# Other SBUF addresses for the split weights, and one queue for the first load and the last store

## The chip, the cores and the metric

The kernel runs on one core of one Trainium2 chip. The metric is the device time of one execution in microseconds; the time before is the median of 3 runs. One core has five engines that run side by side: TensorE (PE in the profile, with its weight loads as PEld), VectorE (DVE), ScalarE (ACT), GpSimd (POOL) and SyncE (SP). Transfers between HBM and SBUF are issued from SP and from ACT and run on 16 DMA engines. SBUF has 128 partitions; an address here is a byte offset within a partition.

## The reference, cut to what matters

```
h = rmsnorm(x) ; proj = h @ w_in                     # 1024 -> q,k,v (512 each), pool (512), gates (2048)
attn   = block attention over q, k, v                # 8 heads of 64; at 256 tokens it is causal attention
pooled = causal means over 2, 4, 8, 16 tokens, one 128x128 map for each of 4 groups, a scale
mixed  = gate0 * (attn @ w_branch_attn) + gate1 * (pooled @ w_branch_pool)
x = x + mixed @ w_out
up = causal_conv3(rmsnorm(x) @ w_up) ; gate, val = split(up)     # 1024 -> 2 x 2816
out = x + (silu(gate) * val) @ w_down                # 2816 -> 1024
```

There are 256 tokens, all in float32.

## The kernel before

**Products.** Each large matrix product is made of three matmuls of type float32r: an operand is split into a high part (`high`, a copy on ACT) and a low part (`low`, the difference, on DVE), and `mm3` adds high x high, high x low and low x high. The weights come in 58 chunks of up to 128 x 2048 numbers (1 MB), in the order that the list `order` writes down: q, k, v, the pool's and the gates' parts, the two branch products, `w_out`, and then `w_up` and `w_down` in turns. `load` fetches a chunk into one of four `raw` buffers from SP's queue; the two q chunks come with x in the tile `xq`. ACT writes the high part into a tile of the pool `whi` and DVE the low part into a tile of `wlo` (four tiles each, taken round by chunk number).

**Matmuls.** In `project` (q, k, v) the activations are the stationary operand, which is loaded into TensorE, and 512 columns of weights stream through as the moving operand: 144 matmuls. In all other float32r products (`feature_tile`, `branch`, `tile_part`, `down`) the weights are stationary and 256 columns of activations (one per token) stream: 2,460 matmuls, of which 1,056 are `w_up`'s (tiles `ps_up`) and 528 are `w_down`'s (tiles `ps_d`). Every matmul has its own weight load, of 128 columns. The remaining 86 matmuls are plain float32 (warm-up, transposes, scores, values, sums).

**Order.** The program order of each engine is fixed by the code; there is no scheduler. All loads stand on SP's queue in one row. The first load is `xq`, in pieces that end after 1, 2, 4, 6 and 8 of the 8 row blocks (`XCUTS`). At the end the eight output blocks of `out_T` are written one after the other, each when DVE has added the residual.

**Addresses.** A tile's address follows from the sizes of what was allocated ahead of it. In the built program all `raw`, `whi` and `wlo` tiles begin at 448 modulo 512, and all activations that a float32r matmul reads (`xhi`, `xlo`, `poolh`, `ath`, `mh`, `hhi`, `ah` and their low parts) at 480. A column slice of either always begins at a multiple of 512 bytes from its tile's start. So the activations stand 32 bytes past the weights, modulo 512, in all 2,604 float32r matmuls.

Of the kernel before, what the change touches and what calls it, by code (L numbers as in the profile page):

```python
# [8 lines left out]
F32 = mybir.dt.float32  # L9
F32R = mybir.dt.float32r  # L10
# [4 lines left out]
P = 128  # L15
S = 256
NT = S // P
D = 1024
KD = D // P
H = 8  # L20
DH = 64
AW = H * DH
# [10 lines left out]
CH = 2048  # L33
# [19 lines left out]
FFN_AHEAD = 6  # L53
KREADY = 0
FIRST = 2
XCUTS = (1, 2, 4, 6, 8)


@with_exitstack
def hybrid_layer_kernel(ctx: ExitStack, tc: tile.TileContext, xq_d, par_d, wkv_d, wpg_d,  # L60
                        wpool_d, wba_d, wbp_d, wout_d, wup_d, wdn_d, out_d):
    nc = tc.nc

    const = ctx.enter_context(tc.tile_pool(name="const", bufs=1))
    raw_p = ctx.enter_context(tc.tile_pool(name="raw", bufs=RAWBUFS))
    whi_p = ctx.enter_context(tc.tile_pool(name="whi", bufs=WBUFS))
    wlo_p = ctx.enter_context(tc.tile_pool(name="wlo", bufs=WBUFS))
    act = ctx.enter_context(tc.tile_pool(name="act", bufs=1))
# [10 lines left out]
    def high(hi, src, scale=1.0):  # L79
        nc.scalar.activation(hi, src, AF.Copy, scale=scale)  # L80
# [16 lines left out]
    order = [("q", None)] * 2 + [("k", wkv_d[c]) for c in range(2)]  # L97
# [10 lines left out]
    raws, his, los = {}, {}, {}  # L108
# [14 lines left out]
    def raw(c, sl):  # L123

        return xq[:, 4 * c + sl.start // 512, S:] if order[c][0] == "q" else raws[c][:, sl]
# [10 lines left out]
    def oldest():  # L136

        return next((c for c in range(len(order)) if c not in spent), len(order))

    def next_high():  # L140
        if at[0] < len(pieces):
            c, sl, first, _ = pieces[at[0]]
            if c - oldest() >= WBUFS:
                return
            at[0] += 1
            if first:
                his[c] = whi_p.tile([P, CH], F32R, tag="whi", name=f"hi_{order[c][0]}{c}")
                los[c] = wlo_p.tile([P, CH], F32R, tag="wlo", name=f"lo_{order[c][0]}{c}")
            high(his[c][:, sl], raw(c, sl))

    def next_low(eager=False):
# [9 lines left out]
    def ahead(upto=0):  # L161

        next_high()
        next_low()
        if at[1] - sum(p[0] < used[0] for p in pieces) < upto:
            next_high()
            next_low()
# [10 lines left out]
    nc.vector.memset(ones, 1.0)  # L178


    xq_all = act.tile([P, KD + KD * (S + AW)], F32, name="xq")
    gmix = xq_all[:, 0:KD]
    xq = xq_all[:, KD:].rearrange("p (k c) -> p k c", c=S + AW)
    xT = xq[:, :, 0:S]
# [5 lines left out]
    cut = 0  # L190
    for k in XCUTS:
        end = KD + k * (S + AW)
        if k == 1:

            nc.scalar.dma_start(out=xq_all[:, KD + S:end], in_=xq_d[:, KD + S:end])
            nc.sync.dma_start(out=xq_all[:, 0:KD + S], in_=xq_d[:, 0:KD + S])
        else:
            nc.sync.dma_start(out=xq_all[:, cut:end], in_=xq_d[:, cut:end])
        cut = end
    nc.scalar.activation(scrap, ones[:, 0:1], AF.Copy)  # L200
    load(2)
# [8 lines left out]

    ident = const.tile([P, P], F32, name="ident")
    make_identity(nc, ident)
    mhalf = const.tile([P, H], F32, name="mhalf")
    nc.gpsimd.memset(mhalf, -0.5)
    mask = const.tile([P, 3, P], F32, name="mask")
# [8 lines left out]
    for k in range(KD):  # L224
        if k == 0:
            nc.vector.tensor_scalar(xhi[:, k, :], xT[:, k, :], gmix[:, k:k + 1], None, op0=ALU.mult)
        else:
            high(xhi[:, k, :], xT[:, k, :], gmix[:, k:k + 1])
        low(xlo[:, k, :], xhi[:, k, :], xT[:, k, :], gmix[:, k:k + 1])
        next_high()  # L230
        next_low(eager=True)
# [199 lines left out]
    def scores(hp):  # L431
        ps = ps2.tile([P, 2, 512], F32, tag="ps2", name=f"ps_s{hp}")
        for j in range(2):
            rows = slice(j * DH, (j + 1) * DH)
            nc.tensor.matmul(ps[:, j, P:3 * P], qT[rows, hp, P:S], kT[rows, hp, :], start=True, stop=True)
            nc.tensor.matmul(ps[:, j, 0:P], qT[rows, hp, 0:P], kT[rows, hp, 0:P], start=True, stop=True)
        sm = tmp.tile([P, 2, 3 * P], F32, tag="big", bufs=4, name=f"sm{hp}")
        nc.vector.tensor_tensor(sm, ps[:, :, 0:3 * P],
                                mask.rearrange("p a b -> p (a b)")[:, None, :].to_broadcast([P, 2, 3 * P]), ALU.add)
        mx = tmp.tile([P, 2, 2], F32, tag="mx", name=f"mx{hp}")  # L440
        for t in (1, 0):
            nc.vector.tensor_reduce(mx[:, t, :], sm[:, :, TOK[t]], axis=AX.X, op=ALU.max)
        nc.vector.tensor_scalar(mx, mx, -(DH ** -0.5), None, op0=ALU.mult)
        sums = tmp.tile([P, 2, 2], F32, tag="sums", name=f"sums{hp}")
        for j in range(2):
            for t in (1, 0):
                nc.scalar.activation(sm[:, j, TOK[t]], sm[:, j, TOK[t]], AF.Exp, bias=mx[:, t, j:j + 1],
                                     scale=DH ** -0.5, accum_out=sums[:, t, j:j + 1])
        rs = tmp.tile([P, 2, 2], F32, tag="rs", name=f"rs{hp}")
        nc.vector.reciprocal(rs, sums)  # L450
        for t in (1, 0):
            n = TOK[t].stop - TOK[t].start
            nc.gpsimd.tensor_tensor(sm[:, :, TOK[t]], sm[:, :, TOK[t]],
                                    rs[:, t, :, None].to_broadcast([P, 2, n]), ALU.mult)
        later(4, weigh, hp, sm)
# [46 lines left out]
    for n in range(2 * KD):  # L502
        if n >= FIRST and (n - FIRST) % 4 == 0:
            scores((n - FIRST) // 4)
        if n == 10:
            pool_maps()
            ahead()
        b, c = n // 2, n % 2
# [123 lines left out]
    def down(i, ms):  # L632
        if i % 2 == 0 and i // 2 not in wd:
            wd[i // 2] = chunk("dn")
        hi, lo = wd[i // 2]
        for m in ms:
            sl = slice((i % 2) * D + m * P, (i % 2) * D + (m + 1) * P)
            o = acc[m // 2][:, (m % 2) * S:(m % 2 + 1) * S]
            first = i == 0 and m % 2 == 0
            nc.tensor.matmul(o, hi[:, sl], acch[i], start=first, stop=False, skip_group_check=True)  # L640
            nc.tensor.matmul(o, hi[:, sl], accl[i], start=False, stop=False, skip_group_check=True)  # L641
            nc.tensor.matmul(o, lo[:, sl], acch[i], start=False, stop=i == KF - 1, skip_group_check=True)  # L642
        if i % 2 == 1 and len(ms) == KD:
            spent.add(next(c for c in his if his[c] is hi))
# [54 lines left out]
    for m in (0, 2, 4, 6, 1, 3, 5, 7):  # L699
        for i in (KF - 2, KF - 1):  # L700
            down(i, (m,))
        o = acc[m // 2][:, (m % 2) * S:(m % 2 + 1) * S]
        nc.vector.tensor_tensor(xT[:, m, :], o, xT[:, m, :], ALU.add)
        if m < 7:
            nc.sync.dma_start(out=out_d[:, m, :], in_=xT[:, m, :])
    for q, rows in ((nc.sync, slice(0, P // 2)), (nc.scalar, slice(P // 2, P))):
        q.dma_start(out=out_d[rows, 7, :], in_=xT[rows, 7, :])


    last = {}  # L710
# [70 lines left out]
```

## Time and profile before

| | |
|---|---|
| median of 3 runs | 347.86 us (347.85 to 348.05) |
| profiled execution | 347.8 us |
| its span on the core (first to last instruction) | 346.0 us |
| mean granted TensorE clock | 0.998 |
| PE busy | 340.3 us (98%), 2,736 matmuls |
| DVE, ACT, POOL busy | 259.3, 198.1, 89.4 us |
| HBM | 62.3 MB, 180 GB/s over the span |

The profiled execution is 1.8 us longer than its span, which is launch and end of the program. Busy time of PE says that a matmul was always in flight, not that it ran at the engine's peak: consecutive matmuls overlap, so the distance from one start to the next is the number to read.

### The profile page before, as it was taken

Reading aid. Unit: us, or ns where it says so; the run is one execution under the profiler, and the core shown is the slowest. Engines: PE = TensorE matmul, PEld = TensorE weight load, DVE = VectorE, ACT = ScalarE, POOL = GpSimd, SP = SyncE. Lnnn points to the kernel's source line nnn. Section 1 sums busy time; section 2 is a strip of 40 time slices with the busy share of each in tenths; the row PEclk is TensorE's granted clock in tenths of the full one; section 3 lists DMA queues with packets and bytes.
Section 4 is the critical chain, followed back from the end, with each engine's and each line's share of the span. In section 5 each row is a group of like instructions: output and inputs, shape, how many; then the busy total and the mean of one; then the engine's idle time right before and its main releaser. Section 6 shows DMA issues by size and latency. Waiting matters only on the chain.

```text
span 346.0 us, 6726 instructions
## 1 busy us (share of the span) xinstructions
PE 340.3 (98%) x2736; PEld 329.3 (95%) x2736; DVE 259.3 (75%) x411; ACT 198.1 (57%) x319; POOL 89.4 (26%) x103
## 2 busy tenths in 40 slices
PE   8999999999999999999999999999999999999995
PEld 7887899999999999999999999999999999999995
DVE  4969889787587585798699977777777777768633
ACT  4956534634748944776467755555556464646420
POOL 1007991112202034123142212121212121221230
PEclk9999999999999999999999999999999999999999
DMA  7985642365272560574257557364646455641003
GB/s 273 421 333 211 217 168 108 150 214 213 86 265 90 230 215 30 172 275 170 116 197 268 183 206 243 122 244 131 236 137 228 145 223 168 209 180 54 0 2 121
DMA packets 10414, 62.76 MB, mean 181 GB/s; under 512 B 1168, under 2 KB 2448, under 8 KB 3472
## 3 DMA queue, kind: packets, MB, share of 16 engines
q1 hardware_dynamic: 10160, 62.01, 49.9%
q8 instruction: 21, 0.34, 0.4%
q10 hardware_dynamic: 224, 0.33, 0.3%
q14 instruction: 9, 0.07, 0.1%
HBM read 61.29 MB, written 1.05 MB: 180 GB/s over the span
## 4 chain that ended last, share of the span: by engine, by line
PE 90%; DMA 5%; DVE 3%; ACT 1%; issue 0%; POOL 0%; SPq 0%; ACTq 0%
PE ps_up L94 12%; PE ps_up L92 12%; PE ps_up L93 12%; PE ps_d L642 6%; PE ps_d L641 6%; PE ps_d L640 6%; PE ps_g L92 5%; PE ps_g L94 4%; PE ps_g L93 4%; DMA raw_k<-in_wkv 3%; PE ps_v L283 3%; PE ps_out L92 2%; PE ps_out L94 2%; PE ps_out L93 2%; PE ps_bp L92 1%; DMA xq<-in_xq 1%
## 5 line engine op out<-in xcount | busy, mean ns | idle before, releaser
L92 PE MATMUL ps_up<-hhi,hi_up 128*128 128x256 f32 x352 | 98.5, 280 | 0.0
L94 PE MATMUL ps_up<-hhi,lo_up 128*128 128x256 f32 x352 | 98.4, 279 | 0.0
L93 PE MATMUL ps_up<-hlo,hi_up 128*128 128x256 f32 x352 | 98.3, 279 | 0.0
L94 PEld LDWEIGHTS ps_up<-hhi,lo_up 128*128 128x128 f32 x352 | 66.2, 188 | 0.2 <-DVE lo_up L84 0.2
L92 PEld LDWEIGHTS ps_up<-hhi,hi_up 128*128 128x128 f32 x352 | 66.2, 188 | 0.0
L93 PEld LDWEIGHTS ps_up<-hlo,hi_up 128*128 128x128 f32 x352 | 66.2, 188 | 0.0
L84 DVE TENSOR_TENSOR lo_up<-raw_up,hi_up 128x1024 fp32r<-128x1024 f32 x44 | 54.5, 1242 | 6.1 <-ACT hi_up L80 6.1
L641 PE MATMUL ps_d<-al,hi_dn 128*128 128x256 f32 x176 | 49.1, 279 | 0.0
L640 PE MATMUL ps_d<-ah,hi_dn 128*128 128x256 f32 x176 | 49.1, 279 | 0.0
L642 PE MATMUL ps_d<-ah,lo_dn 128*128 128x256 f32 x176 | 49.1, 279 | 0.0
L623 POOL TENSOR_TENSOR c_v<-c_g,c_v 128x256 f32<-128x256 f32 x22 | 16.2, 736 | 121.4 <-DVE c_v L606 121.4
L80 ACT ACTIVATE hi_up<-raw_up 128x1024 fp32r<-128x1024 f32 x44 | 44.9, 1044 | 0.0
L92 PE MATMUL ps_g<-xhi,hi_g 128*128 128x256 f32 x128 | 36.5, 285 | 0.0
L93 PE MATMUL ps_g<-xlo,hi_g 128*128 128x256 f32 x128 | 35.7, 279 | 0.0
L94 PE MATMUL ps_g<-xhi,lo_g 128*128 128x256 f32 x128 | 35.7, 279 | 0.0
L80 ACT ACTIVATE ah<-c_v 128x256 fp32r<-128x256 f32 x22 | 9.2, 419 | 45.7 <-POOL c_v L623 45.7
L641 PEld LDWEIGHTS ps_d<-al,hi_dn 128*128 128x128 f32 x176 | 33.1, 188 | 0.0
L642 PEld LDWEIGHTS ps_d<-ah,lo_dn 128*128 128x128 f32 x176 | 33.1, 188 | 0.0
L640 PEld LDWEIGHTS ps_d<-ah,hi_dn 128*128 128x128 f32 x176 | 33.1, 188 | 0.0
L611 DVE TENSOR_TENSOR u_v<-ps_up,R 128x256 f32<-128x256 f32 x22 | 9.3, 422 | 25.7 <-PE ps_up L94 25.6
L84 DVE TENSOR_TENSOR lo_dn<-raw_dn,hi_dn 128x1024 fp32r<-128x1024 f32 x22 | 27.8, 1264 | 0.4 <-ACT hi_dn L80 0.4
L647 POOL TENSOR_TENSOR al<-c_v,ah 128x256 fp32r<-128x256 f32 x22 | 22.8, 1038 | 11.6 <-ACT ah L80 11.6
(182 smaller groups left out, 806.7 us busy)
## 6 DMA issues: line engine op xcount, KB each, us to landing
raw_up<-in_wup SPq DMA_DIRECT2D x22, 1024.0 KB, 4.8
raw_dn<-in_wdn SPq DMA_DIRECT2D x11, 1024.0 KB, 4.7
raw_g<-in_wpg SPq DMA_DIRECT2D x8, 1024.0 KB, 4.8
raw_o<-in_wout SPq DMA_DIRECT2D x4, 1024.0 KB, 4.7
xq<-in_xq SPq DMA_DIRECT2D x3, 768.0 KB, 7.4
raw_v<-in_wkv SPq DMA_DIRECT2D x2, 1024.0 KB, 14.0
raw_p<-in_wpg SPq DMA_DIRECT2D x2, 1024.0 KB, 6.2
raw_bp<-in_wbp SPq DMA_DIRECT2D x2, 1024.0 KB, 4.7
```

The costliest lines, as they stand in the source:

```text
L80: nc.scalar.activation(hi, src, AF.Copy, scale=scale)
L84: nc.vector.tensor_tensor(lo, src, hi.bitcast(F32), ALU.subtract)
L92: nc.tensor.matmul(out, sh, mh, start=start, stop=False, **kw)
L93: nc.tensor.matmul(out, sh, ml, start=False, stop=False, **kw)
L94: nc.tensor.matmul(out, sl, mh, start=False, stop=stop, **kw)
L283: nc.tensor.matmul(pt[t], sx[:, k, t * P:(t + 1) * P], wx[:, sl], start=k == 0 and sx is xhi and wx is hi, stop=k == KD - 1 and wx is lo)
L611: nc.vector.tensor_tensor(u, ps[:, 0:S], R2, ALU.mult)
L623: nc.gpsimd.tensor_tensor(uc[1], g[1], uc[1], ALU.mult)
L640: nc.tensor.matmul(o, hi[:, sl], acch[i], start=first, stop=False, skip_group_check=True)
L641: nc.tensor.matmul(o, hi[:, sl], accl[i], start=False, stop=False, skip_group_check=True)
L642: nc.tensor.matmul(o, lo[:, sl], acch[i], start=False, stop=i == KF - 1, skip_group_check=True)
L647: nc.gpsimd.tensor_tensor(accl[i], act_i, acch[i].bitcast(F32), ALU.subtract)
```

## The change

The weights' high and low tiles get 64 more columns (256 bytes), so that the four tiles of a pool alternate between two addresses modulo 512. A tile `home` of 96 bytes shifts `raw`, `whi` and `wlo`, and 416 bytes ahead of `xq` bring the activations back to 480 modulo 512. `w_down`'s chunks stand 160 bytes further inside their tiles. Apart from that, the first piece of `xq` is one load on SP where it was two on SP and ACT, and the last output block is one store on SP where it was two half stores on SP and ACT.

```diff
+GROWN = 64
+DOWN = 40
+HOME = 24
+LEAD = 104
@@ next_high
-                his[c] = whi_p.tile([P, CH], F32R, tag="whi", name=f"hi_{order[c][0]}{c}")
-                los[c] = wlo_p.tile([P, CH], F32R, tag="wlo", name=f"lo_{order[c][0]}{c}")
+                name = order[c][0]
+                off = DOWN if name == "dn" else 0
+                his[c] = whi_p.tile([P, CH + GROWN], F32R, tag="whi", name=f"hi_{name}{c}")[:, off:off + CH]
+                los[c] = wlo_p.tile([P, CH + GROWN], F32R, tag="wlo", name=f"lo_{name}{c}")[:, off:off + CH]
...
-    xq_all = act.tile([P, KD + KD * (S + AW)], F32, name="xq")
+    xq_all = act.tile([P, LEAD + KD + KD * (S + AW)], F32, name="xq")[:, LEAD:]
...
     for k in XCUTS:
         end = KD + k * (S + AW)
-        if k == 1:
-
-            nc.scalar.dma_start(out=xq_all[:, KD + S:end], in_=xq_d[:, KD + S:end])
-            nc.sync.dma_start(out=xq_all[:, 0:KD + S], in_=xq_d[:, 0:KD + S])
-        else:
-            nc.sync.dma_start(out=xq_all[:, cut:end], in_=xq_d[:, cut:end])
+        nc.sync.dma_start(out=xq_all[:, cut:end], in_=xq_d[:, cut:end])
         cut = end
...
+    home = const.tile([P, HOME], F32, name="home")
+    nc.gpsimd.memset(home[:, 0:1], 0.0)
...
         nc.vector.tensor_tensor(xT[:, m, :], o, xT[:, m, :], ALU.add)
-        if m < 7:
-            nc.sync.dma_start(out=out_d[:, m, :], in_=xT[:, m, :])
-    for q, rows in ((nc.sync, slice(0, P // 2)), (nc.scalar, slice(P // 2, P))):
-        q.dma_start(out=out_d[rows, 7, :], in_=xT[rows, 7, :])
+        nc.sync.dma_start(out=out_d[:, m, :], in_=xT[:, m, :])
```

What this makes of the distance (activations minus weights, modulo 512), counted in the two built programs:

| float32r matmuls | before | after |
|---|---|---|
| all but `w_down`'s, 256 columns | 1,932 at 32 | 1,152 at 448, 780 at 192 |
| q, k, v, 512 columns | 144 at 32 | 72 at 448, 72 at 192 |
| `w_down`'s, 256 columns | 528 at 32 | 192 at 288, 336 at 32 |

The order of TensorE's instructions is the same in both programs: 2,643 rows each, with the same tiles. GpSimd has one memset more. The queues change in two places. This is the start of ACT's program before, where `scrap` is written to load the activation table and `hi_q`, `xhi` are the first high parts:

```order
L776 UNCONDITIONAL_BRANCH
L195 DMA xq<-in_xq 128x512
L200 ACT_TABLE_LOAD
L200 ACTIVATE scrap<-ones 128x1
L80 ACTIVATE hi_q_129<-xq 128x512
L80 ACTIVATE xhi<-xq 128x256
```

And here it is after the change:

```order
L776 UNCONDITIONAL_BRANCH
L201 ACT_TABLE_LOAD
L201 ACTIVATE scrap<-ones 128x1
L84 ACTIVATE hi_q_130<-xq 128x512
L84 ACTIVATE xhi<-xq 128x256
```

The load of the first q weights (512 columns) is gone from ACT; SP's first load grows from 264 to 776 columns in its place. This is the end of SP's program before, from the last weight chunks on:

```order
L121 DMA raw_dn_3692<-in_wdn 128x2048
L121 DMA raw_dn_3792<-in_wdn 128x2048
L705 DMA out_T<-xq 128x256 x7
L707 DMA out_T<-xq 64x256
L776 UNCONDITIONAL_BRANCH
```

And after the change:

```order
L125 DMA raw_up_3628<-in_wup 128x2048
L125 DMA raw_dn_3693<-in_wdn 128x2048
L125 DMA raw_dn_3793<-in_wdn 128x2048
L707 DMA out_T<-xq 128x256 x8
L776 UNCONDITIONAL_BRANCH
```

The store of 64 partitions on SP, and its twin at the end of ACT's program, have become an eighth store of 128 partitions on SP.

## Rows read from the trace of the kernel before

**Rows 1.** The page: span, the share and instructions of each engine, and the 40 slices of PE and of the granted clock (tenths).

```profile
span 346.0 us, 6726 instructions
PE 340.3 (98%) x2736; PEld 329.3 (95%) x2736; DVE 259.3 (75%) x411; ACT 198.1 (57%) x319; POOL 89.4 (26%) x103
PE   8999999999999999999999999999999999999995
PEclk9999999999999999999999999999999999999999
```

**Rows 2.** The page: the chain of work that ended last, its shares by engine.

```profile
PE 90%; DMA 5%; DVE 3%; ACT 1%; issue 0%; POOL 0%; SPq 0%; ACTq 0%
```

**Rows 3.** The timeline of PE (start, length, instruction): 256-column matmuls of `w_up`; 33 matmuls start from the first row up to the last one.

```profile
199.93 0.28 PE L92 MATMUL ps_up<-hhi,hi_up 128*128 128x256 f32 x1
...
203.78 0.28 PE L92 MATMUL ps_up<-hhi,hi_up 128*128 128x256 f32 x1
```

**Rows 4.** The chain in order of time (start, length, what), at the end: 256-column matmuls of `w_down`; 15 lie between the two rows.

```profile
340.09 0.12 PE ps_d L640
...
341.84 0.12 PE ps_d L640
```

**Rows 5.** The timeline of PE: 512-column matmuls of v, in pairs; 18 matmuls start from the first row up to the last one.

```profile
33.51 0.63 PE L283 MATMUL ps_v<-lo_v,xhi 128*128 128x512 f32 x2
...
37.71 0.63 PE L283 MATMUL ps_v<-lo_v,xhi 128*128 128x512 f32 x2
```

**Rows 6.** The timeline of PE where the last matmul of v is followed by the first ones of the pool's part.

```profile
40.74 0.39 PE L283 MATMUL ps_v<-lo_v,xhi 128*128 128x512 f32 x1
40.97 0.28 PE L92 MATMUL ps_u<-xhi,hi_p 128*128 128x256 f32 x1
41.09 0.28 PE L93 MATMUL ps_u<-xlo,hi_p 128*128 128x256 f32 x1
41.21 0.28 PE L94 MATMUL ps_u<-xhi,lo_p 128*128 128x256 f32 x1
41.33 0.28 PE L92 MATMUL ps_u<-xhi,hi_p 128*128 128x256 f32 x1
```

**Rows 7.** Busy time of each engine in stretches (length; PE, PEld, DVE, ACT, POOL busy; granted clock, share of the DMA engines, GB/s).

```profile
1.00:2.00 1.00, 0.95 (x4) 0.95 (x5) 0.00 (x0) 0.82 (x1) 0.92 (x4) 1.00 0.19 14
2.00:3.00 1.00, 1.00 (x7) 1.00 (x6) 0.25 (x1) 0.66 (x2) 0.29 (x2) 1.00 0.64 114
3.00:4.00 1.00, 1.00 (x7) 1.00 (x7) 0.00 (x0) 0.00 (x0) 0.00 (x0) 1.00 0.98 336
4.00:5.00 1.00, 0.83 (x4) 0.54 (x3) 0.57 (x2) 0.42 (x1) 0.00 (x0) 1.00 1.12 394
11.00:14.00 3.00, 3.00 (x15) 2.41 (x14) 3.00 (x7) 3.00 (x6) 0.00 (x0) 1.00 1.05 419
...
32.00:60.00 28.00, 28.00 (x204) 26.09 (x204) 25.34 (x48) 12.16 (x18) 20.45 (x22) 1.00 0.47 171
```

**Rows 8.** The timeline at the start, all engines (idle time before and what ended it in brackets).

```profile
1.25 0.10 POOL L214 MEMSET mhalf<- 128x8 f32 x1
...
2.33 0.25 DVE L223 RECIPROCAL rcnt<-rcnt 128x16 f32<-128x16 f32 x1 [1.33 <-POOL rcnt L220]
...
4.40 0.35 DVE L226 TENSOR_SCALAR xhi<-xq 128x256 fp32r<-128x256 f32 x1 [1.82 <-DMA xq<-in_xq]
4.58 0.63 ACT L80 ACTIVATE hi_q<-xq 128x512 fp32r<-128x512 f32 x1 [1.91 <-DMA xq<-in_xq]
...
5.27 0.79 PE L283 MATMUL ps_q<-hi_q,xhi 128*128 128x512 f32 x1 [0.43 <-DVE xlo L86]
```

**Rows 9.** The chain in order of time, in the first 32 us (start, length, what).

```profile
0.74 3.82 DMA xq<-in_xq
...
4.95 12.00 DMA raw_k<-in_wkv
...
16.98 1.06 ACT hi_k L80
...
29.13 0.67 DVE qg_q L296
29.80 0.14 issue
29.93 2.10 PE ps_v L283 x8
```

**Rows 10.** The timeline where the chain leaves the loads, and where it reaches PE.

```profile
16.98 1.06 ACT L80 ACTIVATE hi_k<-raw_k 128x1024 fp32r<-128x1024 f32 x1 [0.77 <-DMA raw_k<-in_wkv]
...
29.30 0.40 PE L283 MATMUL ps_v<-hi_v,xhi 128*128 128x512 f32 x1
29.93 0.47 PE L283 MATMUL ps_v<-hi_v,xhi 128*128 128x512 f32 x1 [0.24 <-DVE qg_q L296]
30.24 0.40 PE L283 MATMUL ps_v<-hi_v,xlo 128*128 128x512 f32 x1
```

**Rows 11.** DMA issues (count, KB each, median us from issue to landing).

```profile
out_T<-xq SPq DMA_DIRECT2D x7, 128.0 KB, 1.9
xq<-in_xq ACTq DMA_DIRECT2D x1, 256.0 KB, 3.8
raw_pool<-in_wpool SPq DMA_DIRECT2D x1, 256.0 KB, 4.6
xq<-in_xq SPq DMA_DIRECT2D x1, 132.0 KB, 3.6
out_T<-xq SPq DMA_DIRECT2D x1, 64.0 KB, 2.2
out_T<-xq ACTq DMA_DIRECT2D x1, 64.0 KB, 2.5
```

**Rows 12.** The timeline at the end, all engines.

```profile
341.98 0.33 SPq L705 DMA_DIRECT2D out_T<-xq  x1
342.23 0.42 DVE L703 TENSOR_TENSOR xq<-ps_d,xq 128x256 f32<-128x256 f32 x1 [0.27 <-PE ps_d L642]
342.68 0.55 SPq L707 DMA_DIRECT2D out_T<-xq  x1
342.68 0.56 ACTq L707 DMA_DIRECT2D out_T<-xq  x1
```

## The prediction

> **What bounds the kernel now.** I read the page's shares first, then the chain that ended last, then PE's own timeline. PE is busy 340.3 of 346.0 us and its granted clock stands at the upper level, 2.4 GHz, in every slice [rows 1]; 90% of the chain is PE [rows 2]. So from about 30 us on the time is the number of matmuls times the distance between their starts, and everything else counts only at the two ends.
>
> That distance is very regular. 33 matmuls of 256 columns in `w_up` take 203.78 - 199.93 = 3.85 us, 116.7 ns each [rows 3]; 15 in `w_down` take 1.75 us, 116.7 ns again [rows 4]; 18 of 512 columns take 4.20 us, 233.3 ns each [rows 5]. Twice the columns take twice the time, 2.19 columns per ns, although each of them has one weight load of the same 128 columns behind it. At one column per period of 2.4 GHz (an estimate from the clock and that proportion) they would take 106.7 and 213.3 ns, so each 256 columns carry 10.0 ns of excess and each 512 carry 20.0.
>
> At the start two things matter. The chain runs over the load of `raw_k`, which lands at 16.95 us and for which ACT has waited 0.77 us, and from there over ACT and DVE to the eviction of q, which frees a PSUM bank for v at 29.93 [rows 9, 10]. PE starts at 5.27 [rows 8] and stalls just there: 29.30 to 29.93 is 0.63 us where a 512-column matmul takes 0.23, and the next interval of 0.31 has 0.08 more, 0.48 us in all [rows 10]. At the end, DVE's last addition ends at 342.65, the two half stores are issued at 342.68 and land after 2.2 and 2.5 us [rows 11, 12], so at 345.18; 0.8 us of closing work follow to 346.0.
>
> **The change part by part.**
>
> *The addresses.* The order of PE's work is unchanged, so this part can act only through the distance between starts: 2,268 matmuls get another distance between activations and weights, 336 of `w_down`'s keep theirs. The trace of before has only one distance, 32, in all float32r matmuls, so it can't show what 448, 192 and 288 cost, and I bound it. For a gain, the nearest bound is the excess itself: (1,932 + 192) x 10.0 ns + 144 x 20.0 ns = 24.1 us. For a loss I take the same again, a doubled excess, +24.1 us. Between these I take 0, for two reasons from rows. First, if a moving column waited because the next weight load reads near it, the delay would go with the number of weight loads; 512 columns would then carry the same 10 ns as 256, and they carry 20. Second, there is one place where a load stands at another distance: behind the last matmul of v, whose moving operand is weights at 448, TensorE loads weights at 448 too, distance 0. From that matmul to the third one after, 41.33 - 40.74 = 0.59 us pass [rows 6]; one interval of 233.3 and three of 116.7 make 0.583. A load at distance 0 changed nothing that can be seen. The excess looks like a rate at which float32r columns are fed, and that a tile's address won't touch.
>
> The longer tiles add no work for ACT and DVE: they write and read the same 128 x 1024 pieces. The memset of one column on GpSimd stands at the start and makes DVE's first use of GpSimd's work, at 2.33, later by the 0.10 us that such a memset takes; DVE then waits 1.82 us for x anyway, until 4.40 [rows 8]. I cost it at nothing; without that wait it would cost its 0.1 us.
>
> *The last store.* It becomes one store of 128 KB on SP. Seven stores of just that form take 1.9 us from issue to landing; the slower half took 2.5 [rows 11]. The issue is at 342.68 as before, since it waits for the same addition, and SP's queue is free: the seventh store's issue ended at 342.31 [rows 12]. It lands at 344.58 instead of 345.18: -0.6 us. Bounds: the eighth store could take the 2.2 us of SP's half (-0.3), and no store of the seven's form is a ground for more than -0.6.
>
> *The first load.* x and the first q weights, 132 and 256 KB, come as one load of 388 KB on SP. What matters is when it lands and when the stream behind it is saturated. Before, both queues together moved 14, 114 and 336 GB/s in the second, third and fourth us, against 419 later [rows 7]; against 419 throughout, the third and fourth us together lost (305 + 83) / 419 = 0.93 us of transfer. They carried short rows, 1 and 2 KB; the new load has 3.1 KB in each of 128 rows, half as many rows for the same bytes. From the row count the load may be through as soon as the 132 KB load was (3.6 us after its issue, 4.34), and the stream behind it a little earlier. At worst it takes the 4.6 us that 256 KB of `raw_pool` took alone [rows 11], so 5.34, 0.78 later than now (0.74 + 3.82 = 4.56 [rows 9]); PE then starts 0.78 later, of which the 0.48 us that it stalls at 29.3 hide most, and +0.3 is left. At best `raw_k` lands earlier by all that ACT waits for it, -0.77. ACT does nothing else at that time, so that the issue taken from it is worth nothing. I take -0.2.
>
> The Trainium skill, "DMA: Bandwidth & Descriptors", section "Issuing engines are not separate DMA queues", says that transfers issued from several engines run on the same 16 DMA engines and that a second issuer saves only issue time. By that rule the first load's term is about 0 and the sum -0.6; by the ramp in the rows it is -0.2 and the sum -0.8. No row here shows a single 388 KB load at the start.
>
> *Sum.* 0 - 0.6 - 0.2 = -0.8 us on the profiled execution's 347.8, so 347.0. That execution stands 0.06 under the median of 347.86, which is nothing next to the bounds. The likeliest case's own range is 346.4 (-0.6 and -0.8) to 347.8 (-0.3 and +0.3).
>
> **The rivals.**
>
> *The new distance feeds the columns faster.* For it: the excess of 10.0 ns is real, it is there in every stage, and all of it stands at a single distance, so nothing excludes that 32 is a bad one. Against it: its proportion to columns, and [rows 6]. At most it gives 24.1 us, 347.0 - 24.1 = 322.9. DVE would then be near its limit in one stretch, 25.34 of 28 us between 32 and 60 [rows 7], so that a part would be lost there. Half of the excess gives 335. The Trainium skill, "TensorE: Matmul & The Clock Gate", section "Back-to-back issue gap", gives 262 cycles for 256 columns, an estimated 109.2 ns at 2.4 GHz; the trace has 116.7. By that figure the matmuls with a new distance could come down by an estimated 18 us, and the sum would be about 329; whether the address is what keeps them from it, the page doesn't say.
>
> *The new distance feeds them slower.* The mechanism is the same with the other sign: two reads that pass each other undisturbed at 32 meet at 448, 192 or 288, and each meeting holds back the moving columns. For it: nothing in the trace, which has no second distance; against it again [rows 6]. Half of the doubled excess is +12, 359; all of it 371. It decides from about 0.7 ns per 256 columns on: 2,412 times 256 columns (a 512-column matmul counted twice) x 0.62 ns = 1.5 us uses up the 0.8 us gained at the ends and 0.7 more.
>
> *The ends are worth nothing.* The first load lands late and the last store takes 2.2 us: 0 to -0.3, 347.5 to 347.8, no difference that can be told.
>
> **How the numbers follow.** A measurement of this kernel tells about 0.2%, 0.7 us, from no change, so the lines are at 347.16 and 348.56. Unchanged distance between starts: 0.60; of it 0.37 under 347.16 and 0.23 between. Faster columns: 0.24, all under 347.16. Slower columns: 0.16, all above 348.56. That gives 0.61 faster, 0.23 same, 0.16 slower. The predicted time is 347.0. The range from 336 to 350 leaves out the part of the faster case with more than 11 us of gain (0.10) and of the slower one with more than 3 us of loss (0.10).
>
> **What would show it.** In the profile of the changed kernel 33 intervals in `w_up` should take 3.85 us, and those of `w_down` the same in chunks at 288 as in chunks at 32. If they differ between chunks, the addresses matter and the first reason above is wrong; 1 ns is worth 2.4 us. The last store should show 1.9 us from issue to landing. ACT's first high part should start at 4.3 to 4.6 us, ACT's wait for `raw_k` should be 0.77 us or shorter, and PE's stall ahead of v about 0.5 us. A first high part at over 5 us, or a stall that is gone while PE starts late, would make the start term wrong.

## The result, and the profile after

The changed kernel takes 344.38 us (median of 4 runs, 344.26 to 344.75) against 347.87 beside it: ratio 0.990, 95% interval 0.9883 to 0.9918. That is 3.5 us or 1.0% faster, five times what a measurement can tell. Its profiled execution took 344.75 us, the longest of the four; the rows below are from that one. The page and the chain of the changed kernel, which answer to [rows 1, 2]:

```profile
span 343.0 us, 6723 instructions
PE 337.3 (98%) x2736; PEld 326.7 (95%) x2736; DVE 259.9 (76%) x411; ACT 198.2 (58%) x319; POOL 88.6 (26%) x104
PE 85%; DVE 6%; DMA 4%; ACT 2%; SPq 1%; issue 1%; POOL 1%; POOLq 0%; ACTq 0%
```

The span is 3.0 us shorter and PE's busy time, for the same 2,736 matmuls, also 3.0. The next rows give the distance between starts. The timeline of PE after (start, length, instruction): two 256-column matmuls of `w_up` 33 intervals apart, and two of `w_down` 15 apart (the lines are four and three further down in the changed file):

```profile
200.05 0.28 PE L97 MATMUL ps_up<-hlo,hi_up 128*128 128x256 f32 x1
...
203.79 0.28 PE L97 MATMUL ps_up<-hlo,hi_up 128*128 128x256 f32 x1
...
337.63 0.28 PE L645 MATMUL ps_d<-ah,lo_dn 128*128 128x256 f32 x1
...
339.38 0.28 PE L645 MATMUL ps_d<-ah,lo_dn 128*128 128x256 f32 x1
```

33 intervals of `w_up` take 3.74 us, 113.3 ns each, where [rows 3] have 116.7. 15 of `w_down` take 1.75 us, 116.7 ns, exactly as in [rows 4]. So the addresses matter, and `w_down`, at 32 and 288, is the part that did not change.

Where the gain lies is read from the stages' first starts. The same view of both kernels, by tile (duration of a matmul in ns: least, median, most; first and last start). Before:

```profile
L92 PE MATMUL ps_u<-xhi,hi_p x32: 277/280/366, 41.0 to 52.7; 128*128 128x256 f32 x32
L92 PE MATMUL ps_up<-hhi,hi_up x352: 277/280/474, 156.0 to 330.5; 128*128 128x256 f32 x176
```

After:

```profile
L96 PE MATMUL ps_u<-xhi,hi_p x32: 281/281/363, 40.8 to 52.6; 128*128 128x256 f32 x32
L96 PE MATMUL ps_up<-hhi,hi_up x352: 276/276/473, 155.9 to 328.0; 128*128 128x256 f32 x176
```

Up to `w_up`'s first matmul only 0.1 us is gained (156.0 to 155.9); from there to its last 2.4 us (174.5 to 172.1). The duration tells the two apart as well: 281 ns in the pool's part, more than before, and 276 in `w_up`.

**Two rates at one distance.** At 448 and 192 the matmuls run at 113.3 or at 117.8 ns, and stay at one of the two for hundreds of instructions. PE's timeline after, around its only stall in `w_up` and `w_down` that the profile names:

```profile
181.97 0.28 PE L97 MATMUL ps_up<-hlo,hi_up 128*128 128x256 f32 x1
...
183.33 0.28 PE L97 MATMUL ps_up<-hlo,hi_up 128*128 128x256 f32 x1
184.09 0.39 PE L98 MATMUL ps_up<-hhi,lo_up 128*128 128x256 f32 x1 [0.48 <-DVE lo_up L88]
184.31 0.28 PE L96 MATMUL ps_up<-hhi,hi_up 128*128 128x256 f32 x1
...
185.72 0.28 PE L96 MATMUL ps_up<-hhi,hi_up 128*128 128x256 f32 x1
```

12 intervals ahead of the stall take 1.36 us (113.3 ns), 12 behind it 1.41 (117.5), with the same tiles at the same addresses. Tile by tile, of the 44 tiles of `w_up` 41 run at about 113.3 and 3 at 117.8; of the 16 of the gates 7 and 9; the pool's part, `ps_ba` and `w_out` all at 117.8. That is slower than the 116.7 of before, and why the first 156 us brought nothing.

The rows also show a part given back. The interval with the stall is 0.76 us; before, the same matmul came 0.30 us after its predecessor, as PE's timeline of before shows:

```profile
183.65 0.28 PE L93 MATMUL ps_up<-hlo,hi_up 128*128 128x256 f32 x1
183.95 0.39 PE L94 MATMUL ps_up<-hhi,lo_up 128*128 128x256 f32 x1
```

The matmul ahead of it starts at 183.65 before and at 183.33 after, so TensorE was 0.32 us ahead. The one that needs DVE's low part starts at 183.95 and at 184.09, so behind it TensorE is 0.14 us late: 0.46 us is lost there.

**The two ends.** The chain in order of time, after, answers to [rows 9]:

```profile
4.77 12.19 DMA raw_k<-in_wkv
16.98 1.06 ACT hi_k L84
...
29.13 0.67 DVE qg_q L299
29.80 0.14 issue
29.94 2.08 PE ps_v L286 x8
```

The first load did come earlier: in the timeline at the start, to be held against [rows 8], ACT's first high part stands at 4.41 instead of 4.58 and PE at 5.09 instead of 5.27.

```profile
4.41 0.63 ACT L84 ACTIVATE hi_q<-xq 128x512 fp32r<-128x512 f32 x1 [2.18 <-DMA xq<-in_xq]
...
5.09 0.80 PE L286 MATMUL ps_q<-hi_q,xhi 128*128 128x512 f32 x1 [0.26 <-ACT hi_q L84]
```

But `raw_k` lands at 16.96 as before (16.95), ACT waits 0.78 us for it (0.77), and the matmul of v at which the chain reaches TensorE starts at 29.94 (29.93). At the end, the answer to [rows 11] is the DMA issues (KB each, median us from issue to landing), and to [rows 12] the last steps of the chain:

```profile
out_T<-xq SPq DMA_DIRECT2D x8, 128.0 KB, 1.9
xq<-in_xq SPq DMA_DIRECT2D x1, 388.0 KB, 3.6
```

```profile
339.67 0.02 issue
339.69 0.42 DVE xq L706
```

From the end of PE's last matmul to the end of the span it is 343.0 - 339.67 = 3.3 us; before, the last addition starts at 342.23 [rows 12] and 3.8 us are left. So -2.5 us come from PE's intervals, -0.5 from the last store, and 0 from the first load.

### The profile page after: what moved, and what is told of

Its sections match the earlier page's. It is cut to its first block, busy times and chain, and to the rows that moved or that the text cites. A ratio compares the mean times of both kernels' runs of the same rounds, so it can differ in the third digit from the quotient of the medians.

```text
span 343.0 us, 6723 instructions
## 1 busy us (share of the span) xinstructions
PE 337.3 (98%) x2736; PEld 326.7 (95%) x2736; DVE 259.9 (76%) x411; ACT 198.2 (58%) x319; POOL 88.6 (26%) x104
## 4 chain that ended last, share of the span: by engine, by line
PE 85%; DVE 6%; DMA 4%; ACT 2%; SPq 1%; issue 1%; POOL 1%; POOLq 0%; ACTq 0%
PE ps_up L98 10%; PE ps_up L97 10%; PE ps_up L96 10%; PE ps_d L644 6%; PE ps_d L645 6%; PE ps_d L643 6%; PE ps_g L96 5%; PE ps_g L97 4%; PE ps_g L98 4%; DMA raw_k<-in_wkv 4%; PE ps_v L286 3%; PE ps_out L97 2%; PE ps_out L96 2%; PE ps_out L98 2%; PE ps_bp L96 1%; PE ps_ba L97 1%
```

## The experiments

### The two parts of the change, each alone

First the ends alone, on the kernel before:

```diff
-        if k == 1:
-            nc.scalar.dma_start(out=xq_all[:, KD + S:end], in_=xq_d[:, KD + S:end])
-            nc.sync.dma_start(out=xq_all[:, 0:KD + S], in_=xq_d[:, 0:KD + S])
...
+        nc.sync.dma_start(out=xq_all[:, cut:end], in_=xq_d[:, cut:end])
...
+        nc.sync.dma_start(out=out_d[:, m, :], in_=xT[:, m, :])
```

> The kernel before with one first load and one last store on SP, addresses as before (distance 32 everywhere). Theory 1 (the addresses gave most of the gain, the ends about half a us): 347.87 - 0.5 = 347.3, every 256-column matmul still 116.7 ns after the one ahead of it. Rival 2 (the ends and what they trigger at the start gave it): about 344.5.

Measured: 347.37 us against 347.93, ratio 0.9979 (0.9961 to 0.9997); 0.6 us. Both kernels show two levels here. Of the kernel before, ten executions took 347.7 to 348.2 us and six 349.3 to 349.4; with the ends alone nine took 347.2 to 347.5 and three 348.7 to 349.0. Level against level the ends give 0.5 to 0.6 us. What makes the upper level is open: the granted clock was the same, and there is no profile of it. In the profile of the ends alone, at the lower level, `w_up` and `w_down` run at 116.7 ns as before.

Then the addresses alone, which is the changed kernel with the two split transfers of before put back:

> The changed kernel with the first load and the last store split again as before; the addresses of the change. Theory 1: 344.4 + 0.5 = 344.9, with intervals of 113.3 and 117.8 ns at distances 448 and 192 and 116.7 at 32 and 288. Rival 2: about 347.5.

Measured: 345.19 us (344.90 to 345.96), ratio 0.9902 (0.9881 to 0.9923), 2.7 us under 347.93. Together 3.3, and the change gave 3.5. The addresses make the larger part. The profile has the intervals of the changed kernel: 113.3 and 117.8 ns in `w_up`, 116.7 in `w_down`.

### The interval against the distance, by itself

A kernel of its own, which computes nothing of the reference: blocks of 24 matmuls of 256 columns (and of 12 with 512), stationary and moving operand at a chosen distance. Between blocks stand two, three or four transposes in turn.

```diff
+        off = (-8 * i) % P
...
+            for k in range(KD):
+                st = slice(off + k * 256, off + k * 256 + P)
+                mv = slice(k * S, (k + 1) * S)
+                nc.tensor.matmul(ps[:, 0:S], whi[:, st], ahi[:, mv], start=k == 0, stop=False)
...
```

> Computes none of the reference: it measures intervals only. Blocks of 24 matmuls of 256 columns in the order high-high, high-low, low-high, at each of 16 distances (moving minus stationary operand, steps of 32 bytes, modulo 512), three blocks for each distance, each behind 2 to 4 transposes; then 12 matmuls of 512 columns at each distance. Theory 1 (the distance decides, and modulo 256): 116.7 ns at 32 and 288 and one of 113.3 and 117.8 ns, by block, at 448 and 192; equal sets at distances 256 apart. Rival 3 (not the distance but the weights' own address or what stands ahead in the program decides): no dependence on the distance here, since the activations stand at another address than in the kernel, or another pattern than 32 = 288 and 192 = 448.

PE's timeline in it: the 12th and the 24th matmul of a block at distance 0, of one at 32, and of three at 192:

```profile
27.82 0.28 PE L99 MATMUL ps_m<-ahi,wlo 128*128 128x256 f32 x1
29.26 0.28 PE L99 MATMUL ps_m<-ahi,wlo 128*128 128x256 f32 x1
...
37.40 0.28 PE L99 MATMUL ps_m<-ahi,wlo 128*128 128x256 f32 x1
38.80 0.28 PE L99 MATMUL ps_m<-ahi,wlo 128*128 128x256 f32 x1
...
84.92 0.28 PE L99 MATMUL ps_m<-ahi,wlo 128*128 128x256 f32 x1
86.34 0.28 PE L99 MATMUL ps_m<-ahi,wlo 128*128 128x256 f32 x1
...
88.05 0.28 PE L99 MATMUL ps_m<-ahi,wlo 128*128 128x256 f32 x1
89.41 0.28 PE L99 MATMUL ps_m<-ahi,wlo 128*128 128x256 f32 x1
...
91.23 0.28 PE L99 MATMUL ps_m<-ahi,wlo 128*128 128x256 f32 x1
92.59 0.28 PE L99 MATMUL ps_m<-ahi,wlo 128*128 128x256 f32 x1
```

12 intervals take 1.44 us at distance 0 (120.0 ns), 1.40 at 32 (116.7), and at 192 once 1.42 (118) and twice 1.36 (113.3). Here are all distances, moving minus stationary operand, worked out from the starts in the second half of each block, in ns; two or three values where the blocks differ:

| distance modulo 256 | 0 | 32 | 64 | 96 | 128 | 160 | 192 | 224 |
|---|---|---|---|---|---|---|---|---|
| 256 columns | 120.0 | 116.7 | 117.8 | 120.0 | 118.3 to 118.8 | 117.1, 118.5 | 113.3, 117.8 | 118.3 to 118.7 |
| 512 columns | 227 | 233.2 | 228.8 | 233.7 | 232.5 | 234.7 | 233.3 | 232.8 |

Each distance and the one 256 further gave the same. At 192 and at 448, the block behind two transposes ran at 117.8 and those behind three and four at 113.3, so what runs directly ahead seems to choose between the two. The table also gives the kernels' own intervals: 116.7 at 32, and in q, k and v (where the weights move) 233 at 224 before and 228.8 at 64 after. In the probe as built the moving operand of the 256-column blocks begins at 128 modulo 512 and in the kernels at 480, so one distance stands for other addresses in each. The interval followed the distance, and neither operand's own address.

A second kernel of this kind took finer distances:

> Computes none of the reference; the same measurement as the first probe at 16 other distances (moving minus stationary): 16, 48, 80, 112, 144, 176, 208, 240, and 184, 188, 196, 200, 68, 60, 4, 36. If only steps of 32 bytes count (a buffer line of 32 bytes or more), 196, 200 and 208 read as 192 does, with 113.3 in at least one block, and 176 as 160 does. If finer steps count, at least one of them stands apart; a distance with under 113 ns would be a better place than those of the change.

Measured with 256 columns: 120.0 at 4 and at 16, 116.7 at 48, 117.8 at 200, 118.3 to 118.8 at 176, 184 and 188, 118.4 to 119.8 at 196, 120.3 to 121.2 at 36. Nothing was below 113.3, and only 192 reached it: four bytes to either side it is gone. The slowest of all, 36, is four bytes from 32. With 512 columns it was 226.7 at 60, as at 0, and up to 240.2, at 196.

### Distance 0 everywhere

```diff
-GROWN = 64
-DOWN = 40
-HOME = 24
-LEAD = 104
+GROWN = 0
+DOWN = 0
+HOME = 8
+LEAD = 120
```

> The changed kernel with all weights at distance 0 from the activations (no turns, no shift for w_down). Theory 1 with the probe's intervals (120.0 ns for 256 columns at distance 0, 226.7 for 512): 2,460 x (120.0 - 116.7) ns = 8.2 us above the kernel with the ends alone, 347.3 + 8.2 = 355.5, less up to 0.3 for v's matmuls. Rival (the weights' own address or the alternation, not the distance): 344 to 348.

Measured: 354.66 us (354.56 to 355.12), ratio 1.0200 (1.0184 to 1.0215). PE's timeline, 33 intervals in `w_up`:

```profile
202.95 0.28 PE L96 MATMUL ps_up<-hhi,hi_up 128*128 128x256 f32 x1
...
206.91 0.28 PE L96 MATMUL ps_up<-hhi,hi_up 128*128 128x256 f32 x1
```

3.96 us, 120.0 ns each. Addresses alone move this kernel by over 10 us, from 344.4 to 354.7.

### Are the turns needed?

```diff
-GROWN = 64
+GROWN = 128
```

Now all tiles of a pool begin at the same address modulo 512: 448 everywhere, and 288 for `w_down`.

> The changed kernel with 512 bytes more for each tile instead of 256, so that the four tiles do not alternate: distance 448 for all chunks but w_down's, 288 for those. Theory 1 with distances equal modulo 256: intervals and time as in the changed kernel, 344.4 (343.9 to 344.9). Rival (alternating is what brings the gain): back to about 347.3.

Measured: 344.45 us (344.38 to 344.57), ratio 0.9904 (0.9888 to 0.9921). The turns do nothing that can be measured; 448 and 192 are the same modulo 256.

The profiled execution took 344.41 us, like the shorter ones of the changed kernel. In it the first two of the pool's four tiles and the stretch behind the stall ran at 113.3, where the profile of the changed kernel (344.75) has 117.8: some 80 matmuls by 4.4 ns, 0.36 us. The executions of the changed kernel may differ in the same way; only one of them has a profile.

### `w_down` at 448 and 192 too

```diff
-DOWN = 40
+DOWN = 0
```

> The changed kernel with w_down's chunks not shifted, so that they too stand at distances 448 and 192. Theory 1 with the addition that the stream keeps its interval until something breaks it: the 528 matmuls of w_down take 113.3 or 117.8 ns instead of 116.7; if they keep the short one of w_up's, -1.8 us (342.6); if the stream falls into the long one and no block at 32 or 288 brings it back, w_up's 1,056 go from mostly 113.3 towards 117.8 and the time is up to 4.5 us longer than 344.4 (up to 349). Rival 3: 344.4, no change.

Measured: 342.60, 342.99 and 343.08, and 348.47, 348.56 and 348.83 us. Both levels are needed to understand the kernel: which one comes differs from execution to execution, and the median between them means nothing. The granted clock was 0.998 to 1.0 in all six. The profiled execution was of the lower; PE's timeline in `w_down` shows 18 intervals in 2.04 us, 113.3 ns:

```profile
334.64 0.28 PE L643 MATMUL ps_d<-ah,hi_dn 128*128 128x256 f32 x1
...
336.68 0.28 PE L643 MATMUL ps_d<-ah,hi_dn 128*128 128x256 f32 x1
```

Behind the stall at 184 us 849 matmuls of `w_up` and 504 of `w_down` follow; 1,353 x (117.75 - 113.33) ns = 6.0 us, and the levels are 5.6 us apart (342.99 to 348.56). So the upper level fits a stream that leaves the stall at 117.8 and never changes. There is no profile of such an execution, so this is worked out, not seen.

### More stretches at 32

In the changed kernel every group of `w_up` behind a group of `w_down` ran at 113.3. If a stretch at 32 sets that, one ahead of `w_out` and the gates should help these too:

```diff
-                off = DOWN if name == "dn" else 0
+                off = DOWN if name in ("dn", "ba", "p") else 0
```

> The changed kernel with the chunks of the pool's part and of w_branch_attn shifted like w_down's, to distances 288 and 32. Theory 1 with the addition from the runs so far (at 192 and 448 the stream has two lasting intervals, 113.3 and 117.8 ns, and a block at 32 or 288 ahead of it puts it into the short one): the shifted 192 matmuls take 116.7 instead of 117.8, and those of w_out (192, now all at 117.8) and the first of w_up start in the short one: 192 x 4.4 + 42 x 4.4 + 192 x 1.1 ns = 1.2 us, 344.4 - 1.2 = 343.2. If the interval is a matter of the stage and not of what stands ahead of it: only the 192 x 1.1 ns, 344.2.

Measured: 344.24 us (344.18 to 345.08), ratio 0.9903. The time is the one expected if the interval were a matter of the stage, but the profile speaks against that: all eight tiles of `w_out` went from 117.8 to 113.3, as these 33 intervals in 3.74 us show.

```profile
139.81 0.28 PE L96 MATMUL ps_out<-mh,hi_o 128*128 128x256 f32 x1
...
143.55 0.28 PE L96 MATMUL ps_out<-mh,hi_o 128*128 128x256 f32 x1
```

The gates behind the pool's part kept their 7 short tiles of 16. The gain in `w_out` didn't reach the end. This is PE's timeline behind it, with DVE's:

```profile
157.83 0.28 PE L96 MATMUL ps_up<-hhi,hi_up 128*128 128x256 f32 x1
158.81 0.38 PE L97 MATMUL ps_up<-hlo,hi_up 128*128 128x256 f32 x1 [0.71 <-DVE hlo L90]
```

```profile
155.45 0.96 DVE L90 SCALAR_TENSOR_TENSOR hlo<-xq,par,hhi 128x256 fp32r<-128x256 f32 x1
156.34 0.41 DVE L575 TENSOR_TENSOR xq<-ps_out,xq 128x256 f32<-128x256 f32 x1
156.68 1.21 DVE L88 TENSOR_TENSOR lo_up<-raw_up,hi_up 128x1024 fp32r<-128x1024 f32 x1
157.81 0.95 DVE L90 SCALAR_TENSOR_TENSOR hlo<-xq,par,hhi 128x256 fp32r<-128x256 f32 x1
```

DVE goes from one instruction to the next without a gap, 2.36 us a round, and TensorE's matmul on `hlo` comes 0.98 us after the one ahead of it, where 0.11 would do. While DVE sets the pace, a faster TensorE gains nothing there. This profile is of the longest of the four executions (345.08), and TensorE reached the pool's part 0.9 us later in it than in the profile of the changed kernel; how long the wait was in the three at 344.2 wasn't seen.

### Fewer stretches at 32

If a stretch at 32 sets the short interval and it then lasts, `w_down` needs the offset only now and then. Every third chunk:

```diff
-                off = DOWN if name == "dn" else 0
+                off = DOWN if name == "dn" and sum(n == "dn" for n, _ in order[:c]) % 3 == 0 else 0
```

> The changed kernel, but of the 11 chunks of w_down only the first, fourth, seventh and tenth stand 160 bytes further inside their tiles (distance 32 or 288, 192 matmuls); the other seven stand like all other weights, at 448 and 192 (336 matmuls). Theory 1 (a stretch at 32 or 288 is what puts the stream into the short interval; once there it stays at 448 and 192 until TensorE has to wait): 336 matmuls go from 116.7 to 113.3 ns, 1.1 us less than the changed kernel's 344.4, so 343.3, and all runs alike. Theory 2 (the short interval lasts only directly behind each chunk at 32, so that w_up needs one in every round): the rounds without it fall to 117.8 ns in an unforeseeable part, some 600 matmuls by 4.4 ns, so up to 2.7 us more than theory 1: 346.0, with differences from run to run.

Measured: 343.21 us (343.13 to 343.73), ratio 0.9868 (0.9854 to 0.9883), as theory 1 had it. And the first chunk alone:

```diff
-                off = DOWN if name == "dn" else 0
+                off = DOWN if name == "dn" and all(n != "dn" for n, _ in order[:c]) else 0
```

> The changed kernel, but only the first of the 11 chunks of w_down stands 160 bytes further inside its tile (48 matmuls at distance 32 or 288; they are used in two groups, the second behind TensorE's last wait for lo_up at 182 us); all the others stand like the other weights. Theory 1 (one stretch at 32 is enough, and the state lasts until TensorE waits): 480 matmuls go from 116.7 to 113.3 ns, 1.6 us less than 344.4, so 342.8 in every run, without the upper level of 348.6 that the kernel with no such chunk showed in half of its runs. Theory 2 (the state is lost by itself sooner or later, or is drawn at the start of the program): two levels again, 342.8 and 347 to 348.6.

Measured: 342.91 us (342.75 to 342.95), ratio 0.9857 (0.9841 to 0.9874). Once more:

> The same kernel as the one in which only the first chunk of w_down stands 160 bytes further, once more, beside the next one on the same chip. Theory 1 (its second group, at 187.8 us, comes behind TensorE's last wait and sets the stream into the short interval for good): 342.8 in every run. Theory 2 (two levels, and the four earlier runs were lucky): about every second run at 348.6.

Measured: 342.89 us (342.68 to 343.31), ratio 0.9837 (0.9816 to 0.9857). Nine executions of this kernel in all, none at the upper level. At 342.9 us it is 1.5 us ahead of the changed kernel. The first profile left the stall at 113.3 by itself, so it doesn't show what the shifted chunk does. The second one does, in PE's timeline behind the stall at 184.29:

```profile
184.51 0.28 PE L96 MATMUL ps_up<-hhi,hi_up 128*128 128x256 f32 x1
...
187.69 0.28 PE L96 MATMUL ps_up<-hhi,hi_up 128*128 128x256 f32 x1
...
188.39 0.28 PE L643 MATMUL ps_d<-ah,hi_dn 128*128 128x256 f32 x1
...
191.19 0.28 PE L96 MATMUL ps_up<-hhi,hi_up 128*128 128x256 f32 x1
...
194.59 0.28 PE L96 MATMUL ps_up<-hhi,hi_up 128*128 128x256 f32 x1
```

27 intervals behind the stall take 3.18 us, 117.8 ns. Then come the 24 matmuls at 32, and 30 intervals behind them take 3.40 us, 113.3 ns; it stays so to the last matmul.

The counter-test puts the offset on the last chunk alone, where nothing is left to be set:

```diff
-                off = DOWN if name == "dn" else 0
+                off = DOWN if name == "dn" and c == len(order) - 1 else 0
```

> The changed kernel, but only the last of the 11 chunks of w_down stands 160 bytes further inside its tile (48 matmuls, in the last 6 us of TensorE's work); the other ten stand like all other weights. As many matmuls at distance 32 or 288 as in the kernel with only the first chunk shifted, and the same tile sizes. Theory 1 (what matters is a stretch at 32 behind the last wait of TensorE, at 184 us): nothing sets the stream between 184 and 334 us, so two levels again: 342.9, or 1,296 matmuls by 4.4 ns more, 348.6. Theory 2 (one shifted chunk anywhere is enough, for instance because the tiles' places decide): 342.8 in every run.

Measured: 342.84, 342.86, 342.92 and 343.06 us; a fifth execution took 862.32 us at a granted clock of 1.0, which no profile here explains, and is left out. Theory 1 wanted two levels and there was one, as theory 2 had it. In the profile TensorE left its stall at 113.3 by itself and kept it until the last chunk; here are 33 intervals in 3.74 us, in the stretch that no chunk at 32 precedes:

```profile
198.81 0.28 PE L96 MATMUL ps_up<-hhi,hi_up 128*128 128x256 f32 x1
...
202.55 0.28 PE L96 MATMUL ps_up<-hhi,hi_up 128*128 128x256 f32 x1
```

But the shifted chunk can hardly be the reason, since TensorE uses it only after that stretch, and up to it every operand stands where it stands in the kernel without any offset. With the odds of that kernel, three in six, four such draws have a chance of 1 in 16, so this run doesn't decide it. Taken together the two kernels give three in ten, and with these odds nine draws without an upper level, as with the first chunk alone, have a chance of 0.04. That one such chunk is enough in every execution is therefore likely, and not shown; that it can bring the short interval back, the step above shows.

The profiles also show that the choice is not made at the stall alone. Eight of them have the pool's part at 192 modulo 256. In the three in which its first tiles ran at 117.8 (the changed kernel, the addresses alone, and the second one with the first chunk shifted) TensorE left the stall at 117.8 too; in the other five both were 113.3. What links the two was not tested.

## Why the prediction was right and wrong

**Direction and range** held: the forecast was 347.0 with 336 to 350, and the chance for faster 0.61. But it held for the other reason. Of that 0.61 the larger part, 0.37, stood on an unchanged interval and a gain at the ends, and the ends gave 0.5 to 0.6 of the 3.5 us. What happened is the first rival, the new distance feeds the columns faster, at a fifth to a quarter of its price there: 2.5 to 3 us where half the excess would have been 12. That the likeliest case and this rival have the same sign is luck; the range was wide enough to hold both.

**The addresses, taken as 0**, is the step that failed, and both of its reasons with it.

- *The excess goes with columns, so it isn't the weight load.* The rows of before had one distance, and at that one the two widths happen to be in proportion: 10.0 and 19.9 ns over the estimated 106.7 and 213.3. In the table of distances the excess at 0 is 13.3 ns for 256 columns and 13.3 to 14 for 512, the same for each matmul; at 64 it is 11.1 and 15.5. A rule read off one point was no rule.
- *The seam at v, with a load at distance 0, showed nothing.* One load was looked at, in times printed to 10 ns. In a stream the step from 32 to 0 is 3.3 ns per matmul (116.7 to 120.0), worth 7 us over the kernel (354.7 against 347.4 with the ends alone). The seam could not have shown it.

The bounds were sound. A gain up to 24 us and a loss up to 24 us were allowed, and the kernels here lie between 5 us under (342.9) and 7 us over (354.7) the time before. The size is another matter: the excess doesn't vanish at the best distance, it goes from 10.0 to 6.7 ns. The page "TensorE: Matmul & The Clock Gate" of the Trainium skill, section "Back-to-back issue gap", gives 262 cycles for 256 columns, as the gap of an isolated matmul, an estimated 109.2 ns at 2.4 GHz; no distance here reached it.

Three things then cut 6.5 us (1,932 matmuls of 256 columns outside `w_down`, by 3.34 ns) down to 2.5. The stages ahead of `w_up` ran mostly at 117.8, a loss of 1.1 ns each instead of a gain. Three tiles of `w_up` did so too. And DVE's `lo_up` took back 0.46 us in one stall; of DVE as the next limit the prediction had spoken, though in another stretch.

**The test that was named** was badly chosen in its second half: `w_down`'s chunks at 288 and at 32 do agree (116.7), as the prediction wanted of addresses without effect, because 32 and 288 are the same modulo 256. Its first half, 33 intervals in 3.85 us, was the one that spoke: they took 3.74.

**The last store, -0.6**, was right: 1.9 us from issue to landing, 0.5 in the trace, 0.5 to 0.6 in the run with the ends alone.

**The first load, -0.2**, was wrong by its last step. It landed 0.17 us earlier, but the step from there to `raw_k` doesn't exist: `raw_k` lands when the stream of loads has brought it, at 16.96, and v waits on the chain behind it. TensorE, 0.18 us earlier at the start, waits longer ahead of v, 0.90 us from one start to the next instead of the 0.63 of [rows 10], as PE's timeline after shows:

```profile
29.04 0.40 PE L286 MATMUL ps_v<-hi_v,xhi 128*128 128x512 f32 x1
29.94 0.47 PE L286 MATMUL ps_v<-hi_v,xhi 128*128 128x512 f32 x1 [0.50 <-DVE qg_q L299]
```

The prediction had also put down the sum by the Trainium skill, "DMA: Bandwidth & Descriptors", section "Issuing engines are not separate DMA queues", by which the ends are worth 0.6; the run with the ends alone gave 0.5 to 0.6 and agrees.

## What to carry to other kernels

Where TensorE streams matmuls back to back, the interval between starts is a measurable quantity, and operand addresses are among its inputs: try the distance between moving and stationary operand modulo 256 bytes in a small probe before taking an interval as the engine's rate. A proportion seen at a single setting, or a single event read at the resolution of the trace, excludes nothing. When TensorE gets faster, look for the engine whose work is ready just in time: here DVE took back most of what `w_out` gained, and 0.46 us in `w_up`.

## What the runs showed of the hardware that was not expected

- Float32r matmuls of 256 columns start every 113.3 to 121.2 ns, and those of 512 every 227 to 240 ns, by the distance of their operands modulo 256 bytes. The best distance for one width isn't that for the other: 192 gives 113.3 and 233.3, 0 gives 120.0 and 227. Four bytes count: 116.7 at 32 and 120.3 to 121.2 at 36.
- At 192 the same instructions run at 113.3 or at 117.8 ns and keep it for long: 113.3 for 1,300 matmuls in a row in the profile without any offset, 117.8 for some 300 in `ps_ba` and `w_out` of the changed kernel. A wait of TensorE can change it: from 113.3 to 117.8 in the changed kernel, and not in the first run with one shifted chunk.
- Behind each group of `w_down` at 32, and behind `ps_ba` at 32, the stream at 192 ran at 113.3; behind the pool's part at 32 the gates did not. So such a stretch mostly sets the short interval, but what in it does so is open, as is why the kernel without any offset fell into the upper level in three executions of six and the one with only the last chunk shifted in none of four.
